# A gated projection split half and half by output pairs, outputs scaled when they are formed, and residual joins written two tiles at a time

## The chip, the core and the metric

The kernel runs on one core of one Trainium2 chip. The metric is the device time of one execution in microseconds (us). The engines that matter here are TensorE (PE; PEld is its weight load), VectorE (DVE), ScalarE (ACT), GpSimd (POOL) and SyncE (SP), which issues most of the DMAs. Each engine works through its own instructions in their order and waits on semaphores for the others.

## The reference

A trunk of two layers over 256 tokens with 2048 channels, in float32. `x` is the residual stream; every sub-layer has an RMSNorm on its input and one on its output.

```python
def glu(z):                               # the end of the S5 layer
    val, gate = jnp.split(z @ w_glu, 2, axis=-1)     # w_glu: 2048 x 4096
    return val * jax.nn.sigmoid(gate)
x = x + rms(s5(rms(x)), g_mixpost0)       # s5 ends with glu above       -> join 1
x = x + rms(mlp(rms(x)), g_mlppost0)      # mlp: relu(x@w_up)**2 @ w_down -> join 2
k, v = split(rms(x, g_kv) @ w_kv)         # K and V, rotary on k
x = x + rms(diff_attention(rms(x), k, v) @ w_o, g_mixpost1)            # -> join 3
x = x + rms(mlp(rms(x)), g_mlppost1)      #                              -> the finish
```

## The kernel before

The stream lies in SBUF as `h`, 16 tiles of 128 channels x 256 tokens (`NT` = 16, `L` = 256); the output of a sub-layer lies in `y` in the same shape. Float32 weights come in chunks of 128 x 2048 (1 MB, `raw`, L127) and are split into two halves of lower precision: `whi` on ACT (L142) and `wlo` on DVE (L143). The input of a product is split likewise (`xa` and `xb`, eight tiles each; `x2_...` the second such buffer, whose rows the profile calls `x`). One step of the product over 128 channels is then a pair of matmuls, 512 columns with `whi` (L192) and 256 with `wlo` (L193); below it is called a pair step. The last jobs of some products use three matmuls of 256 instead (L188 to L190). A product lands in one of the banks `gb` of PSUM, its second half is copied out by ACT (`cr`, L220) and added on DVE (L203 to L208).

The S5 layer fills the first 245 us. Ten of the 16 output pairs (value and gate) of the first half of the gated projection run in plain float32 beside it (`gemm_f32`, L215, `N32` = 20 jobs). Then come the other six pairs of the first half and all 16 of the second half as split products. The halves meet in accumulators that use `y` and `h` as room, so that `h` must be loaded again after that (four DMAs of 512 KB in `ev_v`, on SP's queue, each behind the pair that frees its quarter).

`Slots` hands out the buffers of raw and split chunks in rotation. At the end of the float32 part two more of each are added (`gx`), behind the two main ones.

A join (`post_norm`) forms 1/rms of `y` over all channels by matmuls with a matrix of ones (L242/L243 or L268 to L272), a square root on ACT (L322) and a reciprocal on DVE (L324). For each of the 16 tiles it then does `t = y * gain * r` (L363), `h += t` (L364), and forms the next product's input: its high half on ACT (L374), its low half on DVE (L375). PE takes up the next product tile by tile as these come, four jobs side by side (`group`); a fifth job needs the bank of the first. The 1/rms of the new `h` is found in one of two ways. `Sums3` collects three sums per tile while `y` is formed, so that only a few operations (`of_h`) are left. Joins 2 and 3 have it. `SumSqPE` squares the new `h` on ACT and sums it by matmuls with 32 columns (L307) in the join. Join 1 has it, since no sum over the input `x` is at hand there. The finish (`finish`, L345 to L352) does the last join and the stores.

The order of instructions on each engine is made by a scheduler from the code, so a changed line can move its neighbours.

## Time and profile before

| | us |
|---|---|
| median of 3 runs (lowest, highest) | 2276.99 (2275.37, 2278.05) |
| profiled execution, its own time | 2273.12 |
| span of its instructions | 2271.3 |
| PE busy / DVE busy / ACT busy / POOL busy | 2226.0 / 1587.5 / 1061.3 / 15.0 |
| granted TensorE clock, mean | 0.994 |

The profiled execution is 3.9 us below the median. Its stages: S5 with the float32 pairs to 265.6 us, split products of the gated projection to 393.5, join 1, first MLP to 1128.0, join 2, K, V and attention to 1436, `w_o` to 1529.8, join 3, second MLP to 2255.6, finish. The span is 1.8 us shorter than the execution's time.

### The profile page before, as it was taken

The page shows a single profiled execution, that of the slowest core. Times are in us where ns is not written, and L with a number is a line of the kernel's source. Part 1 is how long each engine was busy: PE and PEld are TensorE (multiplying, and loading weights), DVE is VectorE, ACT ScalarE, POOL GpSimd, SP SyncE. Part 2 cuts the span into 40 slices and gives each one's busy share as a digit, 9 for nine tenths or more (in the row PEclk, how much of TensorE's full clock was granted, in tenths as well). Part 3 has the DMA queues.
Part 4 walks back from the last instruction along what each step waited for, and adds up shares of the span by engine and source line. Part 5 has one row for each costly group of instructions (what it writes and reads, how often), then busy time and mean ns, then how long its engine had stood idle before and what let it go on. Part 6 is the DMA issues. An engine that isn't in the chain of part 4 may idle for free.

```text
span 2271.3 us, 33587 instructions
## 1 busy us (share of the span) xinstructions
PE 2226.0 (98%) x13701; PEld 1889.3 (83%) x13701; DVE 1587.5 (70%) x2391; ACT 1061.3 (47%) x1628; POOL 15.0 (1%) x26
## 2 busy tenths in 40 slices
PE   8999999999999999999999999998999999999998
PEld 3557788688888888888788888887888888888887
DVE  7999568775566566566898976679756656665665
ACT  4454455544444344344554554555444444444452
POOL 1000000000000000000000000000000000000000
PEclk9999999999999999999999999999999999999999
DMA  7433554356545555554545444454565465455452
GB/s 268 145 134 112 216 198 147 112 186 240 198 173 204 188 183 204 186 185 156 178 154 205 154 171 158 155 179 149 186 240 186 160 223 190 168 205 191 179 186 93
DMA packets 64730, 405.82 MB, mean 179 GB/s; under 512 B 11200, under 2 KB 14016, under 8 KB 17216
## 3 DMA queue, kind: packets, MB, share of 16 engines
q1 hardware_dynamic: 62640, 395.28, 49.2%
q0 software_dynamic: 1792, 6.29, 0.9%
q8 instruction: 108, 1.77, 0.3%
q10 hardware_dynamic: 144, 2.10, 0.2%
q14 instruction: 46, 0.38, 0.0%
HBM read 399.45 MB, written 4.19 MB: 178 GB/s over the span
## 4 chain that ended last, share of the span: by engine, by line
PE 85%; DVE 3%; DMA 1%; ACT 0%; issue 0%; SPq 0%; ACTq 0%
PE gb L192 49%; PE gb L193 25%; PE gb L189 2%; PE gb L188 2%; PE gb L190 2%; PE gb L1041 1%; PE gb L1039 1%; PE gb L1040 1%; PE gb L215 1%; DVE wlo L143 1%; PE mb L307 0%; DVE t L363 0%; PE mb L1000 0%; PE mb L1006 0%; DMA raw<-in_w_glu_dram 0%; DMA raw<-in_w_up_dram 0%
## 5 line engine op out<-in xcount | busy, mean ns | idle before, releaser
L143 DVE TENSOR_TENSOR wlo<-raw,whi 128x2048 fp32r<-128x2048 f32 (+1 forms) x540 | 803.2, 1506 | 505.1 <-ACT whi L142 503.2
L142 ACT CAST whi<-raw 128x2048 fp32r<-128x2048 f32 (+1 forms) x540 | 672.9, 1277 | 613.4 <-PE gb L192 324.7
L192 PE MATMUL gb<-x,whi 128*128 128x512 f32 x2400 | 835.3, 392 | 0.0
L193 PE MATMUL gb<-x,wlo 128*128 128x256 f32 x2400 | 674.8, 281 | 0.0
L192 PEld LDWEIGHTS gb<-x,whi 128*128 128x128 f32 x2400 | 450.5, 188 | 96.5
L192 PE MATMUL gb<-xa,whi 128*128 128x512 f32 x1296 | 461.3, 395 | 10.0 <-DVE xa L375 9.8
L193 PEld LDWEIGHTS gb<-x,wlo 128*128 128x128 f32 x2400 | 452.2, 188 | 0.2
L192 PE MATMUL gb<-xb,whi 128*128 128x512 f32 x1176 | 417.3, 394 | 3.6 <-ACT whi L142 2.1
L193 PE MATMUL gb<-xa,wlo 128*128 128x256 f32 x1296 | 366.2, 283 | 1.3 <-DVE wlo L143 1.3
L193 PE MATMUL gb<-xb,wlo 128*128 128x256 f32 x1176 | 329.9, 281 | 1.6 <-DVE wlo L143 1.6
L192 PEld LDWEIGHTS gb<-xa,whi 128*128 128x128 f32 x1296 | 245.2, 189 | 67.5 <-issue 12.7
L192 PEld LDWEIGHTS gb<-xb,whi 128*128 128x128 f32 x1176 | 221.2, 188 | 55.6 <-DVE xb L375 3.5
L193 PEld LDWEIGHTS gb<-xa,wlo 128*128 128x128 f32 x1296 | 246.1, 190 | 4.8 <-issue 2.5
L193 PEld LDWEIGHTS gb<-xb,wlo 128*128 128x128 f32 x1176 | 222.0, 189 | 2.7 <-DVE wlo L143 2.0
L220 ACT COPY cr<-gb 128x256 f32<-128x256 f32 x323 | 117.6, 367 | 119.8 <-PE gb L193 113.8
L167 ACT CAST x<-t 128x256 fp32r<-128x256 f32 x128 | 51.6, 406 | 190.1 <-DVE t L873 166.2
L652 PE MATMUL gb<-raw,h 128*128 128x512 f32 x256 | 117.5, 606 | 9.7 <-ACT h L427 7.0
L652 PEld LDWEIGHTS gb<-raw,h 128*128 128x128 f32 x256 | 47.2, 192 | 62.4 <-issue 51.7
L205 DVE TENSOR_TENSOR t<-gb,cr 128x256 f32<-128x256 f32 x151 | 62.7, 417 | 34.8 <-ACT cr L220 34.5
L215 PE MATMUL gb<-z,raw 128*128 128x256 f32 x320 | 74.0, 384 | 1.8 <-DMA raw<-in_w_glu_dram 1.6
L168 DVE TENSOR_TENSOR x<-t,x 128x256 fp32r<-128x256 f32 x128 | 53.7, 422 | 30.3 <-ACT x L167 30.2
L215 PEld LDWEIGHTS gb<-z,raw 128*128 128x128 f32 x320 | 59.2, 190 | 12.1 <-issue 2.1
(307 smaller groups left out, 2018.6 us busy)
## 6 DMA issues: line engine op xcount, KB each, us to landing
raw<-in_w_up_dram SPq DMA_DIRECT2D x128, 1024.0 KB, 4.8
raw<-in_w_down_dram SPq DMA_DIRECT2D x128, 1024.0 KB, 4.8
raw<-in_w_glu_dram SPq DMA_DIRECT2D x32, 1024.0 KB, 4.9
raw<-in_w_k_dram SPq DMA_DIRECT2D x16, 1024.0 KB, 4.8
raw<-in_w_q_dram SPq DMA_DIRECT2D x16, 1024.0 KB, 4.8
raw<-in_w_v_dram SPq DMA_DIRECT2D x16, 1024.0 KB, 4.8
raw<-in_w_o_dram SPq DMA_DIRECT2D x16, 1024.0 KB, 4.8
raw<-in_w_in_dram SPq DMA_DIRECT2D x15, 1024.0 KB, 4.8
```

Source lines behind the costliest of these rows:

```text
L142: S.copy(hi[:, c : c + n], raw[:, c : c + n])
L143: V.tensor_tensor(lo[:, c : c + n], raw[:, c : c + n], hi[:, c : c + n].bitcast(F32), op=SUB)
L167: mark[0] = S.copy(dst.hi(dt), src)
L168: mark[1] = V.tensor_tensor(dst.lo(dt), src, dst.hi(dt).bitcast(F32), op=SUB)
L188: T.matmul(ps[:, 0:L], hi[:, c], x.hi(kt), start=f, stop=False)
L189: T.matmul(ps[:, 0:L], hi[:, c], x.lo(kt), start=False, stop=False)
L192: T.matmul(ps, hi[:, c], x.both(kt), start=f, stop=False)
L193: T.matmul(ps[:, L : 2 * L], lo[:, c], x.hi(kt), start=False, stop=l)
L205: V.tensor_tensor(out, ps[:, 0:L], cr, op=ADD)
L215: T.matmul(ps[:, 0:L], w[:, off + kt * P : off + kt * P + P], x[:, kt, :], start=(kt == 0), stop=(kt == nk - 1))
L220: S.copy(cr, ps[:, L : 2 * L])
L652: T.matmul(pss[e], xg[:, kt, e * P : e * P + P], w[:, k4 * 512 : k4 * 512 + 512], start=(kt == 0), stop=(kt == 15))
```

## The change

The gated projection is laid out anew. The first `NP` = 10 output pairs keep two halves: the first in float32, the second as a split product. The other six pairs are no longer halved; their jobs run over all 16 input tiles in one accumulation. `GLU` gives the order of the pairs. The two `gx` buffers of raw and split chunks are put first in the rotation. The four loads of `h` move to POOL's queue, three of them into the S5 stage. `x_sums` forms the token sums of x squared by eight small matmuls, so that join 1 can use `Sums3`; `SumSqPE` goes. In `Sums3.add` and `SumSq.add` ACT scales `y` by its gain when it is formed. The joins then do `y *= r` and `h += y` two tiles at a time, after two single tiles. The finish does likewise with r in PSUM, and two of its additions go to POOL. The extra split buffers for join 3 are opened ahead of `w_o`, and both `pin` calls go.

```diff
-N32 = 20
+NP = 10
+GLU = "6 7 8 9 0 1 15 2 14 3 13 4 12 5 11 10"
...
+            if k and first:
+                self.pools = {name: (p, k), **self.pools}
...
             mark[0] = S.activation(t[:, 0:L], src, AF.Square)
-            S.activation(t[:, L : 2 * L], src, AF.Square, scale=gain(self.g, i))
-            V.scalar_tensor_tensor(t[:, 2 * L : 3 * L], src, gain(self.g, i), h[:, i, :], op0=MUL, op1=MUL)
+            S.activation(src, src, AF.Copy, scale=gain(self.g, i))
+            S.activation(t[:, L : 2 * L], src, AF.Square)
+            V.tensor_tensor(t[:, 2 * L : 3 * L], src, h[:, i, :], op=MUL)
...
-    def finish(gpost, r):
+    def finish(r):
...
             hv = h[:, 2 * i : 2 * i + 2, :]
-            for dt in (2 * i, 2 * i + 1):
-                V.scalar_tensor_tensor(y[:, dt, :], y[:, dt, :], gain(gpost, dt), r, op0=MUL, op1=MUL)
             yv = y[:, 2 * i : 2 * i + 2, :]
-            if i >= len(banks):
-                V.tensor_tensor(hv, hv, yv, op=ADD)
-            else:
+            V.tensor_tensor(yv, yv, bc(r, 1, 2), op=MUL)
+            if i < NADD:
                 T.matmul(banks[i], ident, yv.rearrange("p j t -> p (j t)"), start=False, stop=True)
                 S.copy(hv, banks[i].rearrange("p (j t) -> p j t", t=L))
+            else:
+                (V if i == NT // 2 - 1 else GP).tensor_tensor(hv, hv, yv, op=ADD)
...
-        for dt in range(NT):
-            t = tmp("t", bufs=2)
-            V.scalar_tensor_tensor(t, y[:, dt, :], gain(gpost, dt), r, op0=MUL, op1=MUL)
-            V.tensor_tensor(h[:, dt, :], h[:, dt, :], t, op=ADD)
-            for dst, gpre in outs[:1]:
-                pre(dst, dt, gpre)
-            if ss2:
-                ss2.add(h[:, dt, :])
+        for n in (1, 1) + (2,) * (NT // 2 - 1):
+            hv, yv = h[:, dt : dt + n, :], y[:, dt : dt + n, :]
+            V.tensor_tensor(yv, yv, bc(r, 1, n), op=MUL)
+            V.tensor_tensor(hv, hv, yv, op=ADD)
+            for i in range(dt, dt + n):
+                for dst, gpre in outs[:1]:
+                    pre(dst, i, gpre)
+            dt += n
+        ss.of_h(r)
+        return Known()
...
+        def x_sums():
+            dg = late["p"].tile([P, 2, L], F32, name="dg", tag="rope", bufs=1)[:, :, 0:P]
+            for e in range(2):
+                S.mul(dg[:, e, :], ident, sum_tok[:, e : e + 1])
+            o = late["hss"].rearrange("p (c t e) -> p t e c", t=4, e=2)
+            for e in range(2):
+                for th in range(4):
+                    T.matmul(o[:, 3 - th, 1 - e, :], ones, dg[:, e, 32 * th : 32 * th + 32], start=True, stop=True)
...
+            def reload(k0, k1):
+                GP.dma_start(h[:, k0:k1, :], io["xN"][:, k0 * L : k1 * L].rearrange("p (k t) -> p k t", t=L))
...
+            gemm_f32(first, z32, 8)
+            x_sums()
+            for k0 in (0, 4, 8):
+                reload(k0, min(k0 + 4, 2 * (NT - NP)))
+            raws.set("gx", gx, 2, first=True)
+            splits.set("gx", gx, 2, first=True)
...
+            for n, i in enumerate(order):
+                gemm_b(pair(i), zz, list(range(NT) if i >= NP else range(8, NT)), tail=2 if i == order[-1] else 0)
+                if n == 2 * NP - NT - 1:
+                    reload(2 * (NT - NP), NT)
...
-        ss = SumSq()
-        glu_half(1, ss)
+        ss = Sums3(G_MIXPOST0)
+        glu(ss)
...
-    bs.close()
-    bs, big2 = open_big("big2c")
     ex = with_extra(3, "wb2")
-    ss = post_norm(ss, G_MIXPOST1, [(big1, G_MLPPRE1)])
+    ss = w_o(big2)
+    ss = post_norm(ss, [(big1, G_MLPPRE1)])
```

DVE's order in the second half of the gated projection before, for one output pair (value and gate), from one product's addition to the next.

```order
L207 TENSOR_TENSOR t_2900<-h,cr_2898 128x256
L231 TENSOR_TENSOR acc_sq_2764<-acc_sq_2764,sq_432_2873 128x256
L208 TENSOR_TENSOR t_2900<-t_2900,gb_2881 128x256
L143 TENSOR_TENSOR wlo_3099<-raw_3096,whi_3098 128x2048
L207 TENSOR_TENSOR t_2923<-y,cr_2921 128x256
L208 TENSOR_TENSOR t_2923<-t_2923,gb_2904 128x256
L806 TENSOR_TENSOR y<-t_2923,t_2900 128x8x32
```

The same for a halved pair now, where line numbers are those of the new file.

```order
L210 TENSOR_TENSOR t_2709<-y,cr_2707 128x256
L211 TENSOR_TENSOR t_2709<-t_2709,gb_2690 128x256
L146 TENSOR_TENSOR wlo_2897<-raw_2894,whi_2896 128x2048
L264 TENSOR_TENSOR sq_401_2678<-y,h 128x256
L210 TENSOR_TENSOR t_2732<-y,cr_2730 128x256
L259 TENSOR_TENSOR acc_sq_2505<-acc_sq_2505,sq_401_2678 128x768
L211 TENSOR_TENSOR t_2732<-t_2732,gb_2713 128x256
L806 TENSOR_TENSOR y<-t_2732,t_2709 128x8x32
```

A row with a sum of 256 columns gives way to one of 768 (L231, now L259), and a 256-wide product with `h` is new (L264); the rest is the same.

DVE's order at the start of join 1 before, from the last pair's product to the third tile.

```order
L806 TENSOR_TENSOR y<-t_3618,t_3589 128x8x32
L143 TENSOR_TENSOR wlo_3791<-raw_3788,whi_3790 128x512 x4
L324 RECIPROCAL rst_3655<-rst_3653 128x256
L143 TENSOR_TENSOR wlo_3803<-raw_3800,whi_3802 128x512
L363 SCALAR_TENSOR_TENSOR t_3658<-y,gains,rst_3655 128x256
L363 SCALAR_TENSOR_TENSOR t_3665<-y,gains,rst_3655 128x256
L364 TENSOR_TENSOR h<-h,t_3658 128x256
L364 TENSOR_TENSOR h<-h,t_3665 128x256
L363 SCALAR_TENSOR_TENSOR t_3671<-y,gains,rst_3655 128x256
L375 SCALAR_TENSOR_TENSOR xa<-h,gains,xa 128x256
L364 TENSOR_TENSOR h<-h,t_3671 128x256
L375 SCALAR_TENSOR_TENSOR xa<-h,gains,xa 128x256
```

And now, from the last pair's product to the low halves of tiles three and four.

```order
L806 TENSOR_TENSOR y<-gb_3566,t_3557 128x8x32
L146 TENSOR_TENSOR wlo_3732<-raw_3729,whi_3731 128x512 x2
L264 TENSOR_TENSOR sq_536_3617<-y,h 128x256
L301 RECIPROCAL rst_3647<-rst_3645 128x256
L146 TENSOR_TENSOR wlo_3732<-raw_3729,whi_3731 128x512
L344 TENSOR_TENSOR y<-y,rst_3647 128x256 x2
L345 TENSOR_TENSOR h<-h,y 128x256 x2
L344 TENSOR_TENSOR y<-y,rst_3647 128x512
L355 SCALAR_TENSOR_TENSOR xa<-h,gains,xa 128x256 x2
L345 TENSOR_TENSOR h<-h,y 128x512
```

Gone from the place ahead of the first product with r is the first quarter of a third chunk's `wlo` (`wlo_3803`); the third quarter of the chunk `wlo_3732` stands there now, whose first two quarters come ahead of the reciprocal. Four single steps are the same as before, then each product and addition serves two tiles.

DVE's order at the end of join 2 before, from the last tile's low half to the first addition of a K job (`t_10182`, the one that empties a bank).

```order
L375 SCALAR_TENSOR_TENSOR xb<-h,gains,xb 128x256
L280 TENSOR_TENSOR t_9984<-t_9984,rst_9902 128x256
L143 TENSOR_TENSOR wlo_10029<-raw_10026,whi_10028 128x512
L281 TENSOR_TENSOR hss<-hss,t_9984 128x256
L143 TENSOR_TENSOR wlo_10029<-raw_10026,whi_10028 128x512
L282 TENSOR_SCALAR hss<-hss 128x256
L143 TENSOR_TENSOR wlo_10029<-raw_10026,whi_10028 128x512 x2
L324 RECIPROCAL rst_10174<-rst_10172 128x256
L205 TENSOR_TENSOR t_10182<-gb_10038,cr_10170 128x256
```

And now, up to the same addition (`t_10092`; `x_1303` and `x_1304` are the two halves of the buffer for the input of the query product).

```order
L355 SCALAR_TENSOR_TENSOR x_1303_10186<-h,gains,x_1303_10186 128x256
L286 TENSOR_TENSOR hss<-hss,t_9894 128x256
L355 SCALAR_TENSOR_TENSOR x_1303_10186<-h,gains,x_1303_10186 128x256
L287 TENSOR_SCALAR hss<-hss 128x256
L355 SCALAR_TENSOR_TENSOR x_1303_10186<-h,gains,x_1303_10186 128x256 x2
L301 RECIPROCAL rst_10084<-rst_10082 128x256
L355 SCALAR_TENSOR_TENSOR x_1303_10186<-h,gains,x_1303_10186 128x256
L918 TENSOR_TENSOR rope<-rope,rst_10084 128x256
L919 TENSOR_TENSOR rope<-rope,rst_10084 128x256
L355 SCALAR_TENSOR_TENSOR x_1303_10186<-h,gains,x_1303_10186 128x256
L355 SCALAR_TENSOR_TENSOR x_1304_10187<-h,gains,x_1304_10187 128x256 x7
L208 TENSOR_TENSOR t_10092<-gb_9948,cr_10080 128x256
```

Fifteen of the 16 low halves of the query product's input, which stood behind the K jobs' additions before, now stand ahead of the first of them, and five of the quarter chunks of `wlo` that stood there are gone.

## Rows read from the trace of the kernel before

**Rows 1.** The page: busy time and share; the chain that ended last, by engine.

```profile
PE 2226.0 (98%) x13701; PEld 1889.3 (83%) x13701; DVE 1587.5 (70%) x2391; ACT 1061.3 (47%) x1628; POOL 15.0 (1%) x26
...
PE 85%; DVE 3%; DMA 1%; ACT 0%; issue 0%; SPq 0%; ACTq 0%
```

**Rows 2.** Windows of L192 alone: stretch, its length, busy (count), granted clock, DMA.

```profile
core 0: us, PE busy (x) PEld busy (x), PEclk, DMA share, GB/s
...
393.53:440.00 46.47, 25.71 (x68) 13.02 (x69) 0.93 0.33 121
1128.02:1164.00 35.98, 27.70 (x75) 14.82 (x75) 0.91 0.17 59
1529.75:1566.00 36.25, 25.28 (x65) 13.03 (x65) 0.91 0.31 116
...
1140.00:1164.00 24.00, 23.75 (x69) 12.67 (x68) 1.00 0.25 88
```

**Rows 3.** Timeline of PE at the start of the split products: start, length, idle before.

```profile
267.68 0.73 PE L192 MATMUL gb<-xb,whi 128*128 128x512 f32 x2 [2.12 <-ACT whi L142]
270.00 0.58 PE L193 MATMUL gb<-xb,wlo 128*128 128x256 f32 x1 [1.59 <-DVE wlo L143]
```

**Rows 4.** Timeline of ACT there.

```profile
265.73 1.90 ACT L142 CAST whi<-raw 128x2048 fp32r<-128x2048 f32 x1 [3.21 <-DMA raw<-in_w_glu_dram]
```

**Rows 5.** Windows of PE there: stretch, length, busy (count), granted clock, DMA.

```profile
262.00:266.00 4.00, 3.56 (x17) 1.00 0.99 391
266.00:270.00 4.00, 0.73 (x2) 0.95 0.84 295
270.00:274.00 4.00, 4.00 (x15) 0.62 0.74 260
274.00:278.00 4.00, 4.00 (x25) 1.00 0.60 199
```

**Rows 6.** DVE by line and shape, 280 to 390 us: busy, mean ns of one.

```profile
L143 DVE TENSOR_TENSOR wlo<-raw,whi 128x2048 fp32r<-128x2048 f32 x18 | 41.3, 2292 | 23.9 <-ACT whi L142 23.5 <-PE gb L192 0.5
...
L806 DVE TENSOR_TENSOR y<-t,t 128x256 f32<-128x256 f32 x15 | 10.0, 668 | 0.7 <-ACT t L798 0.2
```

**Rows 7.** DVE by line and shape, 1100 to 1128 us.

```profile
L255 DVE TENSOR_TENSOR acc_sq<-acc_sq,sq 128x768 f32<-128x768 f32 x7 | 6.7, 952 | 0.8 <-ACT sq L258 0.8
```

**Rows 8.** Timeline of DVE in join 2: start, length.

```profile
1149.70 0.42 DVE L364 TENSOR_TENSOR h<-h,t 128x256 f32<-128x256 f32 x1
1150.04 0.48 DVE L363 SCALAR_TENSOR_TENSOR t<-y,gains,rst 128x256 f32<-128x256 f32 x1
1150.43 0.42 DVE L278 TENSOR_TENSOR t<-mb,rst 128x256 f32<-128x256 f32 x1
...
1153.16 0.68 DVE L143 TENSOR_TENSOR wlo<-raw,whi 128x512 fp32r<-128x512 f32 x1
1153.76 0.42 DVE L281 TENSOR_TENSOR hss<-hss,t 128x256 f32<-128x256 f32 x1
...
1156.23 1.74 DVE L324 RECIPROCAL rst<-rst 128x256 f32<-128x256 f32 x1
1157.89 0.35 DVE L205 TENSOR_TENSOR t<-gb,cr 128x256 f32<-128x256 f32 x1
```

**Rows 9.** Timeline of DVE at the start of join 1.

```profile
397.11 1.74 DVE L324 RECIPROCAL rst<-rst 128x256 f32<-128x256 f32 x1
399.53 0.69 DVE L143 TENSOR_TENSOR wlo<-raw,whi 128x512 fp32r<-128x512 f32 x1 [0.68 <-ACT whi L142]
```

**Rows 10.** PE by line and shape in join 1, 393.5 to 440 us.

```profile
L307 PE MATMUL mb<-sq,ones 128*32 128x256 f32 x18 | 6.5, 472 | 6.2 <-ACT sq L302 6.2
L307 PE MATMUL mb<-acc_sq,ones 128*32 128x256 f32 x14 | 4.3, 391 | 0.0
```

**Rows 11.** Timeline of PE: the first steps behind joins 1 and 2.

```profile
403.95 0.80 PE L192 MATMUL gb<-xa,whi 128*128 128x512 f32 x1
...
1136.00 0.77 PE L192 MATMUL gb<-xa,whi 128*128 128x512 f32 x1 [5.22 <-DVE xa L375]
```

**Rows 12.** Timeline of DVE at the start of join 2.

```profile
1131.31 1.74 DVE L324 RECIPROCAL rst<-rst 128x256 f32<-128x256 f32 x1
1132.98 0.63 DVE L143 TENSOR_TENSOR wlo<-raw,whi 128x512 fp32r<-128x512 f32 x1
1133.52 0.87 DVE L363 SCALAR_TENSOR_TENSOR t<-y,gains,rst 128x256 f32<-128x256 f32 x2
```

**Rows 13.** Timeline of DVE at the finish.

```profile
2259.65 5.24 DVE L345 SCALAR_TENSOR_TENSOR y<-y,gains,rst 128x256 f32<-128x256 f32 x13
...
2267.32 0.69 DVE L348 TENSOR_TENSOR h<-h,y 128x512 f32<-128x512 f32 x1
```

**Rows 14.** POOL by line.

```profile
L626 POOL MEMSET M<- 128x2048 f32 x2 | 3.6, 1800 | 0.0
```

More of the change, by code (lines that the diff above doesn't have):

```diff
@@ L783, in glu_half, with glu, pair, get @@
+        def glu(ss):
+            acc_v = [y[:, i, :] for i in range(NP)]
+            acc_g = [y[:, NT - 1 - i, :] if i < NT - NP else h[:, i + NT - NP, :] for i in range(NP)]
+            def reload(k0, k1):
+                GP.dma_start(h[:, k0:k1, :], io["xN"][:, k0 * L : k1 * L].rearrange("p (k t) -> p k t", t=L))
+            def pair(i):
+                full = i >= NP
                 box = {}
-                def get(half, i=i, box=box):
+                def get(vg):
+                    if full:
+                        return chunk(io["w_glu"][2 * i + 1 - vg]) + (0,)
@@ new lines, in glu, with get @@
+            first = []
+            for i in range(NP):
+                box = {}
+                def get(vg, i=i, box=box):
+                    if not box:
+                        box["w"] = chunk(io["w_glu"][i], split=False)
+                    return box["w"], 1024 * vg
+                first.append((lambda f=get: f(0), lambda ps, i=i: added(ps, acc_v[i])))
+                first.append((lambda f=get: f(1), lambda ps, i=i: added(ps, acc_g[i])))
+            gemm_f32(first, z32, 8)
+            x_sums()
@@ new lines, in glu @@
+            for k0 in (0, 4, 8):
+                reload(k0, min(k0 + 4, 2 * (NT - NP)))
+            raws.set("gx", gx, 2, first=True)
+            splits.set("gx", gx, 2, first=True)
+            for dt in range(8):
+                split_to(z1, dt, z32[:, dt, :])
+            order = [int(i) for i in GLU.split()]
+            for n, i in enumerate(order):
+                gemm_b(pair(i), zz, list(range(NT) if i >= NP else range(8, NT)), tail=2 if i == order[-1] else 0)
+                if n == 2 * NP - NT - 1:
+                    reload(2 * (NT - NP), NT)
```

135 lines of the change are left out of this document (49 added, 86 removed).

## The prediction

> **What bounds the kernel now.** The page comes first. PE is busy for 98% of the span and makes up 85% of the chain that ended last [rows 1]. So time can be won where PE works on nothing useful, or works slowly; a shorter job on DVE or ACT is worth something only there. The timeline of PE shows four such places: the start of the split products at 265.6 us, the three joins, and the finish. Between them the products run without a gap.
>
> To price a join I count pair steps in the windows of L192. Steady work is the last row of [rows 2]: 69 steps in 24.00 us, so 0.348 us each. A stretch's loss is its length less its steps times 0.348. Join 1: 46.47 - 68 x 0.348 = 22.8 us. Join 2: 35.98 - 75 x 0.348 = 9.9. Join 3: 36.25 - 65 x 0.348 = 13.6. The reader should see that join 2 is the cheap one. What it still loses is the chain from the last product to the first new step, 1136.00 - 1128.02 = 8.0 us [rows 2, 11], and some 2 us at the lower clock behind it (mean 0.91 over the stretch).
>
> **The start of the split products.** The float32 work ends at 265.56 (267.68 less an idle of 2.12). PE does 0.73 us of work by 270.00: it waits first for ACT's `whi`, then for DVE's `wlo` [rows 3], and ACT had waited for the chunk's DMA [rows 4]. That is 4.44 - 0.73 = 3.7 us. The idle brings the granted clock from 1.00 (the level of 2.4 GHz) to a mean of 0.62 in the next window, part of it at the level of 1.2 GHz, with 15 matmuls where the window after has 25 [rows 5]: 10/25 x 4 = 1.6 us. Now the first two chunks needed go to the `gx` buffers. Their loads stand at the same early places on SP's queue, where before they held chunks for later. Both are split ahead of the end of the float32 work, so PE finds them ready, and the third, which now waits for the main buffer, is wanted 11 us later (behind two output pairs of 16 steps). So -5.3 us.
>
> Against it stand the eight matmuls of `x_sums`, 32 columns each, of which no row exists. Below they cost near nothing; above, as much as L307's rows with 256 columns, two rows a matmul, 10.8 us for 16 [rows 10], so 5.4 us for eight. By columns (32 of 256) it is 0.7. I take 1.5 us, nearer the columns. Net -3.8, bounds -5 to 0.
>
> **The pair jobs.** The split products stay 352 pair steps, since a full pair holds 32 where two halves held 16 each. PE's time is unchanged, and the twelve saved evacuations are not on its path. DVE and ACT get new work, `Sums3`. For a halved pair DVE has one `wlo`, four additions, one product of the gate, the sum with 768 columns in place of 256, and one new product with `h`. Back to back, an instruction starts some 0.08 us before its predecessor's shown end: 0.34 apart for 256 columns, 0.39 for a three-operand one, 0.60 for 512 [rows 8]. So 2.21 + 4 x 0.34 + 0.59 + 0.87 + 0.34 = 5.4 us [rows 6, 7], against 16 x 0.348 = 5.6 on PE. Before it was 4.5. That fits, barely, six times in a row, then alternating with full pairs that have slack. The cover is the four split buffers, about two jobs ahead; without it each 0.1 us over 5.6 costs 1 us in ten halved pairs. I take 0, upper bound +4 (0.4 us of cross waits in each of ten).
>
> The `h` loads leave SP's queue, where the last one stood behind a gate's sigmoid and ahead of join 1's weight loads. On POOL's queue three stand between the loads of `cb` and `rt` in S5, each behind PE's last use of its quarter. I cost that at nothing, because those queued loads themselves have waits about as late; without that cover S5 would be longer by the lateness.
>
> **Join 1.** Removed are the 32 rows of L307, 10.8 us of PE [rows 10], with their squares on ACT; and DVE's block between the reciprocal and the first product with r. There DVE stood from 398.85 (397.11 + 1.74) until the `wlo` at 399.53 was through, 0.68 of it idle for `whi` [rows 9], behind a chunk whose load came late. In its order now a `wlo` stands there too, but its chunk is asked for earlier. Added are two sums of 512 columns at the head, beside the square root, and `of_h`, five short steps, on DVE behind the last tile. Per two tiles DVE does 2 x 0.60 + 2 x 0.39 = 2.0 us where it did 2 x (0.39 + 0.34 + 0.39) = 2.2. Four jobs side by side want 4 x 0.348 = 1.4 us a tile, so PE sets the pace once going. This is join 2's structure as it stands today, so I price it by that: 22.8 - 9.9 = -12.9 us. A check by hand, from the end of the products: reciprocal done at 5.0, as in join 2 (1132.98 - 1128.02), a `wlo` to 5.5 [rows 12], four steps of 0.34, a product and a low half to 7.9, against 403.95 - 393.53 = 10.4 [rows 11]; then 64 x 0.348 = 22.3 us of steps and 2 lost at the lower clock. That is a loss of 9.9, the same. Bounds -8 (the chunk late again, ACT's casts ahead of the first high half) to -14.
>
> **Join 2.** First step as now: four steps at 0.34 in place of two at 0.39 and two at 0.34, then 0.60 in place of 0.39, +0.3 us. PE paces it already. But fifteen low halves of the query's input now stand ahead of the first K addition on DVE: 15 x 0.39 = 5.9 us. All four K jobs now run step by step together, so the fifth waits for that addition. From 1133.5 [rows 12]: 4 x 0.34, 14 x 0.60 for seven pairs of tiles, 16 x 0.39, 1.8 for `of_h`, 5.9, 1.66 for the reciprocal [rows 8], 0.7: DVE is there at 1159.6, PE's fourth job ends at 1136.3 + 22.3 + 2 = 1160.6. A near tie; +0.5, bounds -1 and +3.
>
> **Join 3.** It has the same chain to the first step but fell short of chunks: only some of the four jobs had split weights. With the extra buffers open ahead of `w_o`, four chunks and part of a fifth are split before the join. Priced by join 2: 13.6 - 9.9 = -3.7, bounds -1 to -5.
>
> **The finish.** Sixteen steps of 0.39 and three of 0.60 run from 2259.65 to 2268.01 [rows 13]. Now eight of 0.60 and one addition end at 2259.65 + 4.8 + 0.69 = 2265.1: -2.9 if DVE is last. Two additions go to POOL, one after the other, the first not before the sixth product, 2263.3. POOL's price for 128x512 with two inputs is in no row. Below: DVE's 0.60, which gives 2264.5 and leaves DVE last. Above: its only large row, a fill of 128x2048 in 1.80 [rows 14], which gives 2266.9. I take 1.2, so 2265.7: -2.3, bounds -2.9 and -1.
>
> The Trainium skill speaks against this step. Its page "GPSIMD Engine Reference", section "Engine selection", calls GpSimd about twice as slow as VectorE on two-input elementwise work; "SBUF — State Buffer", section "SBUF: two separate sides", says that a VectorE instruction with two SBUF inputs and a GpSimd one exclude each other for a whole instruction. No run here shows either yet. By both, DVE's last addition could start only behind POOL's second, near 2265.7, and the finish would save 1.7 us instead of 2.3.
>
> **Sum.** -3.8 + 0 - 12.9 + 0.5 - 3.7 - 2.3 = -22.2 us. On the profiled execution's 2273.1 that is 2250.9. It stood 3.9 us under the median, so on the median 2276.99 - 22.2 = **2254.8 us**. What a measurement tells from no change is about 0.2%, 4.6 us.
>
> **Rivals.**
>
> 1. *Join 1 keeps a wait* (0.18). ACT has four casts of a later chunk ahead of the first high half, and DVE a `wlo` in front of the first product. If one of these still waits for its load, 3 us of the late start stay, and the pace of the first tiles with it, about 5: saving 8 instead of 13. For it: the `wlo` is still there. Against it: SP's queue no longer holds it. 2254.8 + 5 = 2260.
>
> 2. *DVE paces the halved pairs* (0.15). Each wait of DVE on ACT's scaled copy lengthens the 5.4 us. At 6.0 to 6.2 us a pair, 4 to 6 us are given back, and DVE enters join 1 behind: 2259 to 2262.
>
> 3. *The early chunks do not help* (0.08). DMA is 0.99 busy at 262 to 266 [rows 5]. The buffers change hands, not the number of loads; if the third chunk comes as late as the first does now, the stall moves there: +3.7 to 5.3, 2259 to 2260.
>
> 4. *Slower than before* (0.04). The sum buffer `sq3` is single, so ACT's square of a pair waits for DVE's sum of the one before, and DVE's product for ACT's copy. Fully in series, DVE's 5.4 us and ACT's cast and five short steps, some 4 us, make 9.4 a halved pair, +3.8 x 10 = +38: 2293. It decides from (22.2 + 4.6) / 10 = 2.7 us a pair, that is at 8.3. Against it: the order interleaves the next pair's additions between these steps.
>
> **How the numbers follow.** The sum as worked out has 0.47: 2250 to 2259 with its small bounds. Better than that (0.08): `x_sums` free and join 1 at its bound, 2247 to 2250. Rivals 1 to 3 lie at 2259 to 2262, two of them together near 2266. The range 2247 to 2267 leaves out the worst pair of rivals and the slower case. Faster by more than 0.2%, below 2272.4: 0.90. Within: 0.06, from three rivals at once or a moderate form of the fourth. Slower: 0.04.
>
> **What would show it.** PE without a gap at 265 us and the clock at 1.00 there; the split products ending near 389.7; no matmul with 32 columns in the first join, and its first step 7 to 8 us behind the last product; join stretches losing about 10 us each; the last DVE step some 5.5 us behind the reciprocal. Wrong, if DVE shows no idle in the halved pairs and PE waits for `wlo` there; if the first K addition comes more than 2 us behind PE; or if the POOL additions end last by far.

## The result and the profile after

| us | before | after |
|---|---|---|
| median (lowest, highest), 4 runs each on one chip | 2277.31 (2275.37, 2278.05) | 2253.72 (2252.67, 2255.59) |
| profiled execution, its own time | 2273.12 | 2253.89 |
| span | 2271.3 | 2251.7 |

The changed kernel takes 0.9897 of the time before [0.9885, 0.9909], 23.6 us less. The forecast was 2254.8. Its sum was made on the profiled execution; there the difference is 19.6 us of span, against 22.2 in the sum. To see which terms hold I cut both traces where the last product of a sub-layer ends on PE: at the start of the first sum behind it or, where that sum waits, at the product's shown end.

| stage | before | after | difference | term |
|---|---|---|---|---|
| start to the end of the gated projection | 393.53 | 390.17 | -3.36 | -3.8 |
| join 1 and the first MLP, to 1128.02 / 1111.78 | 734.49 | 721.61 | -12.88 | -12.9 |
| join 2, K, V, attention, `w_o`, to 1529.75 / 1511.85 | 401.73 | 400.07 | -1.66 | +0.5 |
| join 3 and the second MLP, to 2255.43 / 2236.23 | 725.68 | 724.38 | -1.30 | -3.7 |
| finish, to the end of the span | 15.87 | 15.47 | -0.40 | -2.3 |

The page of the changed kernel first: busy time, and the chain that ended last by engine.

```profile
PE 2217.1 (98%) x13663; PEld 1889.9 (84%) x13663; DVE 1586.1 (70%) x2341; ACT 1088.7 (48%) x1684; POOL 20.0 (1%) x32
...
PE 83%; DVE 3%; DMA 1%; ACT 1%; issue 1%; POOLq 0%; POOL 0%; DVEq 0%; SPq 0%; ACTq 0%
```

Against [rows 1] PE has 38 matmuls and 8.9 us of work fewer: among others the 32 rows of the sums in join 1 are gone, and 16 short ones of `x_sums` have come. It is still the engine that the time goes through.

The start of the split products, PE's timeline of the changed kernel (start, length, idle before; none is shown, so there was none).

```profile
259.14 1.64 PE L767 MATMUL hss<-dg,ones 128*128 128x32 f32 x14
260.62 7.15 PE L218 MATMUL gb<-z,raw 128*128 128x256 f32 x32
267.61 0.30 PE L767 MATMUL hss<-dg,ones 128*128 128x32 f32 x2
267.75 0.48 PE L195 MATMUL gb<-xa,whi 128*128 128x512 f32 x1
```

And windows of all engines in this stage: stretch, its length, busy time and count of each engine, granted clock, DMA share, GB/s.

```profile
core 0: us, PE busy (x) PEld busy (x) DVE busy (x) ACT busy (x) POOL busy (x), PEclk, DMA share, GB/s
266.00:270.00 4.00, 4.00 (x24) 3.55 (x23) 1.94 (x1) 2.17 (x2) 0.00 (x0) 1.00 0.47 162
270.00:274.00 4.00, 4.00 (x25) 3.54 (x24) 1.21 (x4) 2.49 (x5) 0.00 (x0) 1.00 1.01 410
...
267.91:390.17 122.26, 122.26 (x737) 109.25 (x737) 96.56 (x122) 76.70 (x124) 0.55 (x1) 1.00 0.53 188
280.00:300.00 20.00, 20.00 (x118) 17.65 (x117) 18.90 (x27) 13.51 (x25) 0.55 (x1) 1.00 0.76 277
```

Where [rows 3, 5] had two waits and a mean clock of 0.62 behind them, PE now runs on at 1.00. From the end of the float32 work to the end of the projection it has no idle time at all: 122.26 us, and 352 steps of 0.348 are 122.5. The last row is the crowded place: DVE is busy for 18.90 of 20 us in the halved pairs, so it fits, barely.

The joins, as in [rows 2]: windows of the pair steps' first matmul (L195, before L192).

```profile
core 0: us, PE busy (x) PEld busy (x), PEclk, DMA share, GB/s
390.17:436.00 45.83, 38.09 (x104) 20.47 (x104) 0.93 0.33 112
1111.78:1148.00 36.22, 28.29 (x77) 15.14 (x78) 0.95 0.15 56
1511.85:1548.00 36.15, 25.05 (x68) 13.43 (x68) 0.86 0.22 84
```

By the same count (length less steps times 0.348) join 1 loses 9.6 us where it lost 22.8, join 2 loses 9.4 (9.9), and join 3 loses 12.5 (13.6). Join 1 is now as cheap as join 2. Join 3 is not, and the rows below say where its time goes.

Join 1 in the changed kernel, timeline of DVE from the reciprocal, and PE's first step.

```profile
393.00 1.75 DVE L301 RECIPROCAL rst<-rst 128x256 f32<-128x256 f32 x1
...
394.66 0.63 DVE L146 TENSOR_TENSOR wlo<-raw,whi 128x512 fp32r<-128x512 f32 x1
395.20 0.75 DVE L344 TENSOR_TENSOR y<-y,rst 128x256 f32<-128x256 f32 x2
395.87 0.76 DVE L345 TENSOR_TENSOR h<-h,y 128x256 f32<-128x256 f32 x2
...
397.77 0.77 PE L195 MATMUL gb<-xa,whi 128*128 128x512 f32 x1 [3.44 <-DVE xa L355]
```

The `wlo` behind the reciprocal no longer waits for ACT ([rows 9] had 0.68 there), and the first step stands 7.6 us behind the last product, against 10.4 in [rows 11].

Join 3 in the changed kernel, timeline of the engines ahead of its first step.

```profile
1506.72 2.19 ACT L145 CAST whi<-raw 128x512 fp32r<-128x512 f32 x4 [2.46 <-DMA raw<-in_w_up_dram]
1507.38 2.50 DVE L146 TENSOR_TENSOR wlo<-raw,whi 128x512 fp32r<-128x512 f32 x4 [1.96 <-ACT whi L145]
...
1512.75 0.95 DVE L259 TENSOR_TENSOR acc_sq<-acc_sq,sq 128x768 f32<-128x768 f32 x1
...
1513.76 0.70 PE L273 MATMUL mb<-acc_sq,ones 128*128 128x256 f32 x2 [1.91 <-DVE acc_sq L259]
...
1514.63 0.62 ACT L145 CAST whi<-raw 128x512 fp32r<-128x512 f32 x1 [0.93 <-DMA raw<-in_w_up_dram]
1515.16 0.41 ACT L261 ACTIVATE sq<-y 128x256 f32<-128x256 f32 x1
...
1516.88 0.48 ACT L299 ACTIVATE rst<-mb,gains 128x256 f32<-128x256 f32 x1 [0.39 <-PE mb L274]
...
1522.17 0.76 PE L195 MATMUL gb<-xa,whi 128*128 128x512 f32 x1 [2.38 <-DVE xa L355]
```

Read it from the bottom. The first step is 10.3 us behind the last product (7.6 in join 1), the square root 5.0. Ahead of the root stands ACT's last square of `y`, and ahead of that a cast of a weight chunk that has nothing to do with the join, waiting 0.93 us for its DMA. Before it, PE's sum waited 1.91 us for DVE's running sum. That wait begins at the top: the third weight chunk's load came late (2.46 us of idle on ACT, 1.96 on DVE), its casts and low halves stood ahead of the work on the last tiles of `y`, and low halves of the fourth chunk stood between that work and the running sum.

### The profile page after: what moved, and what is told of

Same layout as the page of the kernel before. It is cut to its first block, busy times and chain, and to the rows that moved or that the text cites. A ratio compares the mean times of both kernels' runs of the same rounds, so it can differ in the third digit from the quotient of the medians.

```text
span 2251.7 us, 33494 instructions
## 1 busy us (share of the span) xinstructions
PE 2217.1 (98%) x13663; PEld 1889.9 (84%) x13663; DVE 1586.1 (70%) x2341; ACT 1088.7 (48%) x1684; POOL 20.0 (1%) x32
## 3 DMA queue, kind: packets, MB, share of 16 engines
q8 instruction: 107, 1.75, 0.3%
## 4 chain that ended last, share of the span: by engine, by line
PE 83%; DVE 3%; DMA 1%; ACT 1%; issue 1%; POOLq 0%; POOL 0%; DVEq 0%; SPq 0%; ACTq 0%
PE gb L195 47%; PE gb L196 25%; PE gb L192 2%; PE gb L191 1%; PE gb L193 1%; PE gb L1050 1%; PE gb L1049 1%; PE gb L1048 1%; PE gb L218 1%; DMA raw<-in_w_o_dram 1%; DVE wlo L146 1%; ACT whi L145 1%; DMA raw<-in_w_up_dram 0%; PE mb L1015 0%; PE mb L1009 0%
## 5 line engine op out<-in xcount | busy, mean ns | idle before, releaser
L195 PE MATMUL gb<-x,whi 128*128 128x512 f32 x2400 | 835.2, 392 | 0.0
L195 PEld LDWEIGHTS gb<-x,whi 128*128 128x128 f32 x2400 | 450.5, 188 | 95.5
L195 PE MATMUL gb<-xa,whi 128*128 128x512 f32 x1328 | 472.7, 395 | 9.9 <-DVE xa L355 9.3
L195 PE MATMUL gb<-xb,whi 128*128 128x512 f32 x1168 | 412.3, 392 | 0.0
L196 PE MATMUL gb<-xa,wlo 128*128 128x256 f32 x1328 | 375.1, 282 | 0.0
L195 PEld LDWEIGHTS gb<-xa,whi 128*128 128x128 f32 x1328 | 251.6, 190 | 68.2 <-issue 12.4
L195 PEld LDWEIGHTS gb<-xb,whi 128*128 128x128 f32 x1168 | 219.2, 188 | 48.4
L196 PEld LDWEIGHTS gb<-xa,wlo 128*128 128x128 f32 x1328 | 252.9, 190 | 0.1
```

The lines of the kernel that those rows point to most:

```text
L195: T.matmul(ps, hi[:, c], x.both(kt), start=f, stop=False)
L196: T.matmul(ps[:, L : 2 * L], lo[:, c], x.hi(kt), start=False, stop=l)
```

## The experiments

The first five undo one part each or do one part alone. A difference from the changed kernel compares medians of separate batches; the kernel before, timed in each batch, had medians of 2277.31, 2277.72, 2276.17 and 2276.59, so differences of a microsecond or two are weak by themselves. No run undoes the scaled outputs, the loads of `h` on POOL's queue, the earlier buffers for join 3, or the dropped `pin` call. Of the two `pin` calls, both named as gone above, only `pin(2, 1)` at the end of each MLP went; `pin(1, 1)` stays.

**The extra buffers last again**, in the changed kernel.

```diff
-            raws.set("gx", gx, 2, first=True)
-            splits.set("gx", gx, 2, first=True)
+            raws.set("gx", gx, 2)
+            splits.set("gx", gx, 2)
```

> The changed kernel with the two extra weight buffers put last in the rotation again; nothing else differs. Theory (the stall at the start of the split products is set by which buffer the first chunk needed gets): PE's idle of about 4 us between the float32 part and the first split product returns, the clock falls behind it, and the time rises by 3.7 to 5.3 us over the changed kernel (about 2253.7), to 2257 to 2259. Rival (the loads are the same, so the stall was hidden or only moved): within 1 us of the changed kernel.

Measured 2258.89 us, 0.9918 of before [0.9904, 0.9931]: 5.2 more than the changed kernel. PE's timeline of this kernel at the start of the split products:

```profile
267.50 0.74 PE L195 MATMUL gb<-xa,whi 128*128 128x512 f32 x2 [0.45 <-ACT whi L145]
269.82 0.39 PE L196 MATMUL gb<-xa,wlo 128*128 128x256 f32 x1 [1.59 <-DVE wlo L146]
```

The two waits are back, 0.45 and 1.59 us, and so is the lower clock (0.60 in the window from 270 us). So the order of the buffers, not the new job order, had removed them. By stages, the start is 3.3 us longer than in the changed kernel (the projection ends at 393.45) and join 1 with its MLP 1.8; the second part was not forecast, and its cause stays open.

**The extra buffers first, alone**, in the kernel before (and `Slots.set` as in the change).

```diff
-                raws.set("gx", gx, 2)
-                splits.set("gx", gx, 2)
+                raws.set("gx", gx, 2, first=True)
+                splits.set("gx", gx, 2, first=True)
```

> The kernel before with one part of the change alone: the two extra weight buffers put first in the rotation. Theory: the stall of 3.7 us and the 1.6 us at the lower clock go, and nothing is added, so 5 us less than the kernel before (about 2277.3), near 2272. Rival (the third chunk is then late, or the gain needs the new layout): less than 2 us.

Measured 2269.00 us, 0.9964 [0.9952, 0.9977]: 8.7 us less by the medians, 8.2 by the ratio, more than the 5 expected. The profiled execution, at 2272.08, is the longest of its five. In its profile the projection ends at 388.28, 5.25 earlier than before, which is the 5.3 of the term. At the end of `w_o` only 1.64 of it is left. DVE and PE in the K products of this kernel:

```profile
1166.84 0.42 DVE L944 TENSOR_TENSOR lp<-lamv 128x256 f32<-128x256 f32 x1 [2.20 <-DMA lamv<-in_lamv_dram]
...
1169.86 0.58 PE L195 MATMUL gb<-xa,wlo 128*128 128x256 f32 x1 [2.73 <-DVE wlo L145]
```

DVE stood 2.20 us for a small load of attention parameters (`lamv`), with the low halves of PE's next chunk queued behind it. In this execution the wait, with a granted clock of 0.73 and 0.84 in the two windows of 4 us from 1168 us, takes back most of what the start had won; the median of the five does not show such a loss. It led to the three `lamv` runs below.

**The old sums in join 1**, in the changed kernel (`SumSqPE` put back, with its squares in the join; `Sums3` in the gated projection replaced by `SumSq`).

```diff
+        ss2 = None if isinstance(ss, Sums3) else SumSqPE()
...
+                if ss2:
+                    ss2.add(h[:, i, :])
...
-        ss = Sums3(G_MIXPOST0)
+        ss = SumSq(G_MIXPOST0)
```

> The changed kernel with join 1 by squares of the new stream in the join again (16 squares on ACT, 32 rows of 32-column matmuls on PE), and with one sum in place of three in the gated projection. The new layout, the scaled outputs and the tile-pair steps stay; the sums of the input are still formed and not used. Theory (the matmuls of the join are most of its loss): the part from the end of the gated projection to the end of the first MLP grows by 9 to 11 us, the time by as much, to 2263 to 2265. Rival (the late start behind the reciprocal, 2.8 us, and the steps are the loss): 1 to 3 us more.

Measured 2263.34 us, 0.9938 [0.9926, 0.9950]: 9.6 more than the changed kernel. PE by line and shape in its join 1:

```profile
L312 PE MATMUL mb<-sq,ones 128*32 128x256 f32 x18 | 6.5, 472 | 4.8 <-ACT sq L307 4.8
L312 PE MATMUL mb<-acc_sq,ones 128*32 128x256 f32 x14 | 4.3, 391 | 0.0
```

The 32 rows cost the 10.8 us of [rows 10] again. The stage of join 1 is 11.5 us longer (389.16 to 1122.30), that of join 3 2.5 us shorter, where PE's sum no longer waits; the time rises by 9.6. The squares and their sums in join 1 were the largest part of the change.

**Joins one tile at a time**, in the changed kernel.

```diff
-        for n in (1, 1) + (2,) * (NT // 2 - 1):
+        for n in (1,) * NT:
```

> The changed kernel with one tile at a time in all three joins; the outputs are still scaled when they are formed. Theory (the four jobs on PE set the pace of a join, 1.4 us a tile against 1.07 on DVE): within 1 us of the changed kernel. Rival (the pairs are what makes the joins shorter): 24 pairs at some 0.14 us, over 3 us slower.

Measured 2255.20 us, 0.9909 [0.9894, 0.9924]: 1.5 more than the changed kernel, and the two intervals overlap. In the profile the stage of join 1 is 4.2 us longer (388.57 to 1114.36), but that of join 3 2.1 shorter (1515.35 to 2237.68): its sum waits 0.20 us for DVE instead of 1.91. In these rows the pairs are worth something at join 1, and about half of that is hidden again by the wait at join 3. The time lies between the theory (within 1 us) and the rival (over 3 us), and does not separate them.

**The finish without POOL**, in the changed kernel.

```diff
-                (V if i == NT // 2 - 1 else GP).tensor_tensor(hv, hv, yv, op=ADD)
+                V.tensor_tensor(hv, hv, yv, op=ADD)
```

> The changed kernel with the finish's two POOL additions done by DVE, so that DVE has eight products and three additions there. Theory (POOL's two additions, 2.94 us in the changed kernel's trace, and the stores behind them end the kernel): DVE ends at about the time of POOL's end, 11 us behind the last product, and the last store follows sooner; 0.5 to 1.5 us faster than the changed kernel. Rival (POOL takes work off the engine that ends last): 1 us slower.

Measured 2253.68 us, 0.9893 [0.9878, 0.9909], 0.04 from the changed kernel. Neither the gain nor a loss came. DVE's last addition ends 11.0 us behind the last product, as POOL's did, so POOL is neither a help nor a hindrance there.

**The first store earlier**, in the changed kernel: the first pair of tiles is added on DVE, five more pairs by PE and ACT, one on POOL and the last on DVE.

```diff
-        for i in range(NADD):
+        for i in range(1, NADD + 1):
...
-            if i < NADD:
-                T.matmul(banks[i], ident, yv.rearrange("p j t -> p (j t)"), start=False, stop=True)
+            if 0 < i <= NADD:
+                T.matmul(banks[i - 1], ident, yv.rearrange("p j t -> p (j t)"), start=False, stop=True)
...
-                (V if i == NT // 2 - 1 else GP).tensor_tensor(hv, hv, yv, op=ADD)
+                (GP if i == NT // 2 - 2 else V).tensor_tensor(hv, hv, yv, op=ADD)
```

> The changed kernel with the finish's first tile pair added by DVE in place of PE and ACT, so that its store can go some 0.8 us earlier; the sixth pair goes by PE and ACT. Theory (the eight stores saturate the DMAs from the first one on, so the first store sets the end): the end comes 0.6 to 1 us earlier behind the last product than in the changed kernel (15.5 us). Rival (the last additions set the end): no change.

Measured 2253.94 us, 0.9904 [0.9891, 0.9918]: no change. The first store is issued 6.1 us behind the last product instead of 6.8, yet the span ends 15.8 behind it instead of 15.5. The first store does not set the end. Its timeline has a pair of rows on what the prediction could not show, an addition on POOL beside one on DVE:

```profile
2246.20 1.27 POOL L327 TENSOR_TENSOR h<-h,y 128x512 f32<-128x512 f32 x1 [1952.74 <-DVE y L322]
...
2246.70 1.33 DVE L327 TENSOR_TENSOR h<-h,y 128x512 f32<-128x512 f32 x1
```

**The fifth chunk of the second MLP later**, in the changed kernel: `rstd_of` marks the square root and the reciprocal, and the split of the fifth chunk is issued behind them.

```diff
-        S.activation(sd, ps, AF.Sqrt, bias=eps, scale=scale)
+        mark[0] = S.activation(sd, ps, AF.Sqrt, bias=eps, scale=scale)
...
-        V.reciprocal(r, sd)
+        mark[1] = V.reciprocal(r, sd)
...
+    pin(4, 1)
```

> The changed kernel with the split of the fifth weight chunk of the second MLP held behind join 3's reciprocal. In the changed kernel's trace ACT's first cast of that chunk waits 0.93 us for its DMA ahead of the square of the last tile of y, and the square root comes 5.0 us behind the last product (2.6 before the change). Theory (that cast is why join 3 gained 1.3 us and not 3.7): the square root comes 1 to 2 us earlier and the time falls by 1 to 2 us, to about 2252. Rival (join 3 is set by the sums on DVE, or the chunk is then missed as the fifth job's): no gain, or 1 us slower.

Measured 2251.62 us (2251.16 to 2253.00), 0.9895 [0.9882, 0.9909]. That is the lowest median of all, 2.1 less than the changed kernel's, but by the ratios (0.9895 and 0.9897) only 0.5 less, with intervals that overlap almost whole. Timeline of its join 3:

```profile
1512.97 0.95 DVE L259 TENSOR_TENSOR acc_sq<-acc_sq,sq 128x768 f32<-128x768 f32 x1
...
1513.97 0.70 PE L273 MATMUL mb<-acc_sq,ones 128*128 128x256 f32 x2
1514.34 0.42 ACT L261 ACTIVATE sq<-y 128x256 f32<-128x256 f32 x1
...
1516.00 0.47 ACT L299 ACTIVATE rst<-mb,gains 128x256 f32<-128x256 f32 x1 [0.26 <-PE mb L274]
...
1521.28 0.76 PE L195 MATMUL gb<-xa,whi 128*128 128x512 f32 x1 [4.29 <-DVE xa L355]
```

No cast with a DMA wait stands ahead of the last square, and the square root comes 2.1 us behind the last product's shown end (1513.90) instead of 5.0. Last product to last sum of the second MLP is 721.5 us here (to 2235.37), 4.2 less than before, near what the prediction had wanted of join 3. But part of this is again that PE's sum did not wait in this execution. The run with the first store earlier separates the two: up to the finish its code is the changed kernel's, and there the sum waited only 0.33 us (shown end of the last product: 1513.39). Timeline of ACT and PE in its join 3:

```profile
1516.45 0.46 ACT L299 ACTIVATE rst<-mb,gains 128x256 f32<-128x256 f32 x1
...
1521.88 0.77 PE L195 MATMUL gb<-xa,whi 128*128 128x512 f32 x1 [3.44 <-DVE xa L355]
```

Its square root is 3.1 us behind the last product and its first step 8.5; with the chunk held back they are 2.1 and 7.4. So about 1 us of the join is shown for holding the chunk; a gain in the time is likely but not clear of noise.

**Three runs on the `lamv` load, in the kernel before.** First its issue, with that of the mask, moved from SP's queue to POOL's.

```diff
-        DMA.dma_start(lamv, dview(io["lamv"], 0, [[0, P], [HD, 4], [1, HD]]))
+        GP.dma_start(lamv, dview(io["lamv"], 0, [[0, P], [HD, 4], [1, HD]]))
```

> The kernel before with the loads of the mask and of the lambda vectors issued by POOL in place of SP. In two traces DVE waits there for the second of them with a weight chunk's wlo queued behind it; PE idles 1.0 us in the one and 2.7 us with a drop of the clock in the other. Theory (this wait, of varying length, costs the kernel before some 4 us in most executions, and its going is the part of the gain that the two profiled executions do not show): 3 to 5 us faster than the kernel before (about 2277.7), and less spread. Rival (it is the profiled 1 us and no more): 0 to 1 us.

Measured 2279.85 us, 1.0017 [1.0008, 1.0026]: slower by a little, against the expectation. In its timeline the load lands 5.8 us behind its issue (3.5 in the kernel before), and DVE's wait grows:

```profile
1172.25 0.42 DVE L942 TENSOR_TENSOR lp<-lamv 128x256 f32<-128x256 f32 x1 [3.03 <-DMA lamv<-in_lamv_dram]
...
1175.27 0.58 PE L193 MATMUL gb<-xa,wlo 128*128 128x256 f32 x1 [3.79 <-DVE wlo L143]
```

It serves as a dose all the same. In four executions of the kernel before and its variants DVE's wait for `lamv` was under 0.1, 0.57, 2.20 and 3.03 us; PE's idle time behind it 1.03, 1.45, 2.73 and 3.79; and the stage from join 2 to the end of `w_o` 401.73, 402.34, 405.38 and 407.17. A long wait lengthens the stage, by more than PE's idle time: in the POOL run the clock from 1165 to 1190 us was 0.86, in the kernel before 1.00. Second, the work on `lamv` placed behind the low halves of the query's input, so that no low half waits behind it.

```diff
-        V.scalar_tensor_tensor(dst.lo(dt), h[:, dt, :], gain(gpre, dt), dst.hi(dt).bitcast(F32), op0=MUL, op1=SUB)
+        mark[1] = V.scalar_tensor_tensor(dst.lo(dt), h[:, dt, :], gain(gpre, dt), dst.hi(dt).bitcast(F32), op0=MUL, op1=SUB)
...
-        V.tensor_tensor(lp, lamv[:, 0:2, :], lamv[:, 2:4, :], op=MUL)
...
+        with tc.issue_after(mark[1].ins):
+            V.tensor_tensor(lp, lamv[:, 0:2, :], lamv[:, 2:4, :], op=MUL)
```

> The kernel before with DVE's product of the lambda vectors (and the three short steps behind it) held until the query product's input is formed; its load stays on SP's queue. With that load on POOL's queue the load took longer, PE idled 3.8 us instead of 1.0, and the time rose by 3.7 us, so the wait is on the path. Theory (DVE's wait for that load is the whole of it): PE no longer idles in the K product, 3 to 5 us faster than the kernel before, and the stretch from join 2 to the end of the output product takes near 400 us in place of 401.7 to 405.4. Rival (the weight chunk itself is late there): PE idles as before, less than 1 us.

Measured 2273.79 us, 0.9989 [0.9980, 0.9998], 2.8 less than the before of its batch (2276.59; 2.5 by the ratio), a little under the 3 to 5 expected. But the theory's signs did not come: the stage took 402.09 us, not near 400, and PE still idles for the same `wlo`. PE's rows at this place in the kernel before, in this run, and in the third run:

```profile
1173.02 0.39 PE L193 MATMUL gb<-xa,wlo 128*128 128x256 f32 x1 [1.03 <-DVE wlo L143]
1175.02 0.38 PE L193 MATMUL gb<-xa,wlo 128*128 128x256 f32 x1 [0.54 <-DVE wlo L143]
1164.89 0.39 PE L195 MATMUL gb<-xa,wlo 128*128 128x256 f32 x1 [0.93 <-DVE wlo L145]
```

In the last two DVE has no wait for `lamv` and works without a gap ahead of that `wlo`. So 0.5 to 1 us of PE's idle time there comes from the work that stands ahead of the `wlo` on DVE; the load adds to it only where it lands late. Third, this with the extra buffers first.

> The kernel before with two edits together: the extra weight buffers first in the rotation, and DVE's product of the lambda vectors held back. Theory (the parts add): the gains of the two alone, some 5 and 4 us, make 8 to 10 us, near 2268; what the changed kernel has beyond that is joins 1 and 3 less the small matmuls. Rival (the first edit already took the second's gain by moving the order): no more than the first alone (8.7 us at its first timing).

Measured 2266.38 us, 0.9961 [0.9948, 0.9975], 10.2 less than that before (8.9 by the ratio). Its stage to the end of `w_o` took 401.74 us, as in the kernel before. Beside the extra buffers alone it is 2.6 us less by the medians, but only 0.7 by the ratios, whose intervals overlap, so theory (the gains add) and rival (no more than the buffers alone) are not separated.

**The kernel before once more**, for a second profile.

> The kernel before, once more, for a second profiled execution. Theory (the wait in the K product differs from one execution to the next, and the first profiled execution, 3.9 us under the median, caught a short one): PE idles more than 1.0 us in the K product here, the clock may drop, and the stretch from join 2 to the end of the output product is longer than 401.7 us. Rival: the stretch is the same, and the 4 us lie elsewhere.

Its execution took 2272.22 us, again 4.4 under the median. DVE's wait for `lamv` was 0.57 us, the stage 402.34 (401.73), both longer as expected, yet the time was shorter. So the wait does vary between executions of one program, but it did not make this one long. PE at the start of the split products in this execution:

```profile
267.77 0.74 PE L192 MATMUL gb<-xb,whi 128*128 128x512 f32 x2 [1.75 <-ACT whi L142]
270.09 0.38 PE L193 MATMUL gb<-xb,wlo 128*128 128x256 f32 x1 [1.59 <-DVE wlo L143]
```

The two waits are there as in [rows 3], but from 270 to 274 us the granted clock was 1.00 with 23 matmuls, where [rows 5] had 0.62 with 15.

## Why the prediction was right, point by point

**The start of the split products.** Term -3.8, measured -3.36. The gain was sized well: between the end of the float32 work and the end of the projection the kernel before took 127.97 us (from 265.56), the changed one 122.26, so -5.7 where I had -5.3. The eight matmuls of `x_sums` are 16 rows and took 1.94 us by their shown lengths instead of 1.5, and S5 itself came 0.4 late in this execution. The size has some luck in it. The clock's share, 1.6 us, was missing in the second execution of the kernel before. Over the profiled executions the projection ended at 392.25 to 395.45 us where this stage was as before (four), and at 388.56 to 391.30 in the changed kernel and four runs that have its stage unchanged. The means, 393.6 and 390.2, differ by 3.4.

**The pair jobs.** Term 0, measured 0: PE has no idle time there. DVE's 94% in the window from 280 us is near the 5.4 us against 5.6 that had been worked out (96%). Rivals 2, 3 and 4 did not come.

**Join 1.** Term -12.9, measured -12.88. Pricing it by join 2 was enough, since it became join 2's structure; the first step at 7.6 us (7.9 in the check by hand) and the loss of 9.6 (9.9) agree separately. The experiment with the old sums gives 11.5 of the stage, and 9.6 of the time, to those. That term and measurement agree to 0.02 is luck: in three more profiled executions with the same join 1 the stage was 721.9 to 722.3 us, which would have been -12.6 to -12.2. Rival 1 did not come here.

**Join 2.** Term +0.5, measured -1.66. The near tie on DVE went PE's way: the first K addition came at 1142.94, near the time worked out (1159.6, less the 16.2 by which this join began earlier), and PE shows no wait in the K products. For the first step the prediction has +0.3, but its own durations give +0.1 (1.36 + 0.60 against 1.46 + 0.39); it came 7.8 us behind the last product instead of 8.0. What the term left out is a wait that PE had there before: 1.03 us for DVE's `wlo`, the first of the three rows shown with the `lamv` runs. It is gone, and with a join that loses 9.4 instead of 9.9 it makes 1.5 of the 1.66. The load of `lamv` is not the reason, since DVE waited under 0.1 us for it in that execution, and without any wait for it PE still idled 0.54 and 0.93 us. What is left is DVE's new order, in which the low halves of the query's input, and the five quarter chunks of `wlo`, have changed places; which line did that, the dropped `pin` call among them, was not tried. The load has moved too. Timeline of SP's queue and DVE in the changed kernel:

```profile
1152.26 0.42 SPq L948 DMA_DIRECT2D lamv<-in_lamv_dram  x1
...
1158.42 0.42 DVE L951 TENSOR_TENSOR lp<-lamv 128x256 f32<-128x256 f32 x1
```

It is issued 6.2 us ahead of its use, where before it was issued at 1166.49 for a use at 1170.00, so the long waits of other executions are less likely here. A sum over DVE's durations doesn't see such a load.

**Join 3.** Term -3.7, measured -1.30. This is a term that was mis-sized, and the step that failed is "the same chain to the first step". Timeline of the kernel before, the square root and the first step of join 3:

```profile
1532.37 0.47 ACT L322 ACTIVATE rst<-mb,gains 128x256 f32<-128x256 f32 x1
...
1537.79 0.76 PE L192 MATMUL gb<-xa,whi 128*128 128x512 f32 x1 [4.62 <-DVE xa L375]
```

There the root stood 2.6 us behind the last product and the first step 8.0; now they stand 5.0 and 10.3 behind it. Behind the first step the join lost 5.6 us before (13.6 less 8.0) and 2.2 now (12.5 less 10.3). So what the prediction wanted of the earlier buffers came, -3.4, and a chain to the first step that is 2.3 us longer took most of it back. In ACT's order four chunks and half of a fifth stand ahead of the root, but the third's load was late, and the fifth's cast stood ahead of the join's last square and waited for its load. That is rival 1's mechanism at another join. How long the chain waits differs between executions with the same code there: PE's sum waited 1.64 to 1.94 us in three, 0.33 in one and not at all in the run with the old sums in join 1, whose first step was 7.7 us behind the last product though the fifth chunk's cast still stood ahead of the square. Holding that chunk back shortens the chain by about 1 us. What makes the third chunk's load late, and with it the sum, was not tried and stays open.

**The finish.** Term -2.3, measured -0.40, mis-sized too. Up to the end of the additions it went nearly as worked out: DVE had ended 12.6 us behind the last product [rows 13], now POOL ends 11.0 behind it, -1.6. Timeline of the changed kernel:

```profile
2240.45 4.87 DVE L322 TENSOR_TENSOR y<-y,hss 128x512 f32<-128x512 f32 x8
...
2243.05 5.26 SPq L328 DMA_DIRECT2D out_dram<-h  x8
...
2244.27 2.94 POOL L327 TENSOR_TENSOR h<-h,y 128x512 f32<-128x512 f32 x2 [1951.51 <-DVE y L322]
...
2245.36 0.73 DVE L327 TENSOR_TENSOR h<-h,y 128x512 f32<-128x512 f32 x1
```

Two steps that I had left out take back the rest. The last of SP's eight store issues ends 1.1 us behind POOL (0.4 behind DVE before), and the stores then take 3.4 us to the end (2.9 before). The same 2.1 MB come in less time: DMA share 0.99 at 322 GB/s in the window from 2244 to 2248, against 0.90 at 291 GB/s from 2263 to 2267 before. Neither run on the finish won anything, and whether the issues or the DMA engines are the limit stays open.

POOL's two additions took 1.27 and 1.70 us, the second longer while DVE's addition ran; I had 1.2 each. In the run with the first store earlier one addition takes 1.27 on POOL, and 0.68 on DVE when it is alone. The Trainium skill's factor of about two ("GPSIMD Engine Reference", "Engine selection") agrees with that: 1.9 times. In the same run DVE's addition beside POOL's took 1.33, and it ended 0.56 us behind it; the Trainium skill's "SBUF: two separate sides" in "SBUF — State Buffer", by which the two exclude each other, agrees too. By both pages of the Trainium skill the finish would have saved 1.7, with DVE's addition behind POOL's second. The additions' end did come 1.6 us earlier, but in another order: DVE's addition was through first, POOL's second ended last, and the stores took most of the gain.

**The time itself.** The terms missed by 2.6 us in sum, yet the median came within 1.1 of the forecast. That is luck of the base: the profiled execution before lay 3.9 us under its median, as the prediction said, while that of the changed kernel lies on it (2253.89 and 2253.72), so 4 us of the measured gain are in no term. The clock on record points to where they are. Of 39 timed executions of the kernel before in the later batches, the four with a mean granted clock of 0.995 took 2271.5 to 2273.9 us, the 17 with 0.992 took 2276.6 to 2280.4. The two profiled ones have 0.994 and 0.995; the changed kernel has 0.995 and 0.996 in its four. So the profiled executions of the kernel before are merely near the short end, and most lose more at the lower clock. One place where that varies is the start of the split products: in the windows from 270 and 274 us the clock was 1.00 and 1.00 in one execution, 0.62 and 1.00 in another, 0.50 and 0.76 in the profiled one of the run with the `lamv` work held back, each time behind two waits of 1.4 to 2.1 us; the changed kernel has no such waits. Another is a long wait for `lamv`. That the buffers first won 8.2 us alone, 3 more than their term, fits the first. How the 4 us divide was not shown, since the other executions have no trace.

## What to carry to other kernels

Price a stage by its nearest finished sibling in the same trace: join 1 rebuilt like join 2 lost what join 2 loses, to some tenths of a microsecond. Compare a profiled execution's time and mean clock with those of the others before a sum is made on it. On engines that work in order, look at which weight chunk's cast or low half stands ahead of a norm's last square or sum, and whether its load has landed; an early chunk is good only if it can't make the norm wait. A shorter last computation is worth little when the stores behind it take longer for it.

## What the runs showed of the hardware that I had not expected

- A small load in a busy stage takes long to land, and not the same time in each execution: `lamv` landed 3.5 to 5.2 us behind its issue in five executions of the kernel before and its variants on SP's queue, and 5.8 us behind it in the one on POOL's.
- The price of a narrow float32 matmul does not go by its columns: the 16 rows of `x_sums` with 32 columns took 1.94 us, 0.12 each, and the 32 rows with 256 columns between them 7.15, 0.22 each. An eighth of the columns costs half.
- Similar idle times of PE are followed by different clocks. In the kernel with the extra buffers last, idle times of 0.45 and 1.59 us, from 267.05 to 269.82 us, were followed by a mean granted clock of 0.60 over the window from 270 to 274 us, which held 16 matmuls where a window at 1.00 holds 25. In the second execution of the kernel before, idle times of 1.75 and 1.59 us were followed by a clock of 1.00.
